# Attention in a two-layer trunk: rotation sums in token order, a third place for the swapped halves, and output products begun during the last head

## The chip, the cores and the metric

One core of one Trainium2 chip (trn2) runs the kernel. The metric is the device time of one execution in microseconds (us). The engines are TensorE (PE in the profile; PEld is its weight load), VectorE (DVE), ScalarE (ACT), GpSimd (POOL) and SyncE (SP), which issues nearly all DMAs of this kernel. The profile also gives the clock that TensorE was granted, as a share of 2.4 GHz: 1.00 is 2.4 GHz and 0.50 is 1.2 GHz.

## The reference

A trunk of two layers over 1024 tokens and 1024 channels. Layer 0 mixes tokens by a gated linear recurrence, layer 1 by dilated attention; a SwiGLU feed-forward layer (FFN) follows each, and a norm stands ahead of each part and at the end. The change touches layer 1's mixer:

```
DILATED_GROUPS = ((128, 1), (512, 4), (2048, 16))     # (window, dilation), 4 heads of 128 each

def apply_rope(x, cos, sin):
    x1, x2 = jnp.split(xf, 2, axis=-1)
    out = jnp.concatenate([x1 * cos - x2 * sin, x2 * cos + x1 * sin], axis=-1)

def dilated_attention_mixer(u, w_qkv, w_out, cos, sin):
    q = apply_rope(qkv[:, :, 0], cos, sin)
    k = apply_rope(qkv[:, :, 1], cos, sin)
    v = qkv[:, :, 2]
    for gi, (window, dilation) in enumerate(DILATED_GROUPS):
        o_g, lse_g = dilated_window_group(q[:, :, hs], k[:, :, hs], v[:, :, hs], window, dilation)
    o = jnp.stack(outs, axis=2)
    alpha = jax.nn.softmax(lse, axis=2)               # shares of the three groups
    o = (o * alpha[..., None]).reshape(B, S, ATTN_WIDTH)
    return o @ w_out

h = x
for layer in range(DEPTH):
    h = h + mixer(rmsnorm(h))
    h = h + (silu(gate) * up) @ w_down                # gate, up = rmsnorm(h) @ w_in
```

## The kernel before

Channels lie on the 128 partitions and tokens along the row. Every float32 product is made of three products of split operands (a high and a low part): a copy on ACT makes the high part, a subtraction on DVE the low one. In the profiled run the stages are: recurrence until 480 us, its output projection until 620, FFN 0 until 1290, values for all heads until about 1437, the twelve attention heads until 1756, the seam where the heads run out and the output projection starts, until 1804, the rest of that projection until 1920, and FFN 1 until the end.

A head is named by its number: n is group times 4 plus j, and the heads run in the order 0, 4, 8, 1, 5, 9, 2, 6, 10, 3, 7, 11 (j is the outer loop), so a10 is followed by a3 and a11 is the last. Head n's q and k come from seven products, a{n}a to a{n}g (twelve matmuls each, a Strassen-like scheme over the two token halves). Four of them need a copy first: L744 copies product a's sum into the bank in which c goes on adding, so **c cannot start before L744**; L750 does the same for e; L747 copies product b's sum into `s5`, half of a tile `sz{n}`.

`attn_qk` then rotates four quarters with `rope`, in the order q's first token half, k's second, q's second, k's first. A rotation copies the lower 64 rows of a quarter to the upper 64 and back (L780, L781, ACT) into `z`, the other half of `sz{n}`; `z` is multiplied by the sine table (L784), the quarter by the cosine table (L783 or L786), and L787 adds the two into the result tile `aq{n}` or `ak{n}`. Quarters 2 and 3 need `s5` added first (L778). In groups 1 and 2 the result has its tokens sorted by their remainder mod 4 or 8, "permuted" below; L778 writes permuted, so the copies L780 and L781 of quarters 2 and 3 read permuted and write back in token order, and the cosine product works on permuted data. All four rotations use the one `z`.

The steps of a head that follow are put between the products of the next: `later(n, step)` files a step under a clock that `tick()` counts, seven to a head. They are: scores (L846, into banks `as`) with their maxima (L849, DVE, into `st`) in two parts; `ng` (L856, DVE), the negative maxima; the exponentials (L858, ACT), which need `ng`; transposes (L891, PE) with copies (L892, ACT); the value products (L901) with copies (L903 or L907, ACT). After each third head the softmax sums are brought to a common layout by DMAs through memory (`dn`, `cm`), group shares are worked out (`ae`, `dw`), and the **merge** multiplies finished outputs by them: reloads L955 and L956 into `mg`, multiply L962, write L963 to `od`.

At the seam the nine merged outputs of j below 3 are loaded from `od` into tiles `am`, split into `aov0` to `aov8` (L144 on ACT, L145 on DVE) and multiplied by output weights `n3w` (L124, L125, L127): `part_out(d, lo, hi)` runs products lo to hi of unit d, six matmuls each, and two units d0 and d1 are begun among the last head's steps. The last three outputs, `aov9` to `aov11`, follow the chain `dn`, `cm`, `ae`, `dw`, a load `wb` (L1022) and a multiply (L1023); after them come products 9 to 11 of d0 and d1, and `mixer_out` with the other units.

What the engines run in order is not the written order: the framework's list scheduler sets an order for each engine from dependencies, priorities by place in the program, and its own cost estimates; an engine then takes its instructions strictly in that order. Tiles of one tag rotate through a fixed number of places: "vc" tiles hold `sz`, `aq`, `ak`, `am` and others, "wx" has two. `lm` is a mask of the recurrence in layer 0.

Of the kernel before, what the change touches and what calls it, by code (L numbers as in the profile page):

```python
# [8 lines left out]
F32 = mybir.dt.float32  # L9
F32R = mybir.dt.float32r  # L10
U8 = mybir.dt.uint8
# [4 lines left out]
P = 128  # L16
T = 1024
# [3 lines left out]
NH = 12  # L21
# [8 lines left out]
NMASK = 3 * len(STAGES) + 1  # L30
# [10 lines left out]
def trunk_kernel(ctx, tc, x, cols, consts, w_in, w_hout, w_qkv, w_aout, w_ffn, w_down, out):  # L41
    nc = tc.nc
# [8 lines left out]
    def big(tag, name, dt=F32):  # L51
        return gp.tile([P, T], dt, tag=tag, name=name, bufs=slots[tag])
# [4 lines left out]
    def mmps(name):  # L57
        return pmm.tile([P, 512], F32, tag="mm", name=name)
# [4 lines left out]
    def hs(hh):  # L63
        return slice(hh * 512, hh * 512 + 512)
# [74 lines left out]
    def split(src, tag, name, scale=None, cuts=((0, T),)):  # L139
        hi = big(tag, f"{name}h", F32R)  # L140
        lo = big(tag, f"{name}l", F32R)
        for a, b in cuts:
            if scale is None:
                nc.scalar.copy(hi[:, a:b], src[:, a:b])  # L144
                nc.vector.tensor_sub(lo[:, a:b], src[:, a:b], hi[:, a:b].bitcast(F32))  # L145
            else:
                nc.scalar.activation(hi[:, a:b], src[:, a:b], AF.Copy, scale=scale)
                nc.vector.scalar_tensor_tensor(lo[:, a:b], src[:, a:b], scale, hi[:, a:b].bitcast(F32), ALU.mult, ALU.subtract)
        return hi, lo
# [64 lines left out]
        nm.begin()  # L214
        rb = nm.finish("vb")

    lm = cp.tile([P, NMASK, 2, P], U8, name="lm")
    for i0 in range(0, NMASK, 8):
        n = min(8, NMASK - i0)
        lmf = big("ws", f"lmf{i0}")  # L220
# [498 lines left out]
    def later(n, step):  # L719
        steps.setdefault(n, []).append(step)  # L720
# [8 lines left out]
    mark = {}  # L729
# [38 lines left out]
    nc.sync.dma_start(ev0, consts[:, K_DIAG:K_DIAG + P].rearrange("(r i) c -> i r c", r=2))  # L768
    nc.vector.tensor_copy(even.rearrange("p (i r) -> p r i", r=2), ev0.rearrange("p (r i) -> p r i", r=2))

    def rope(t, ps, s5, hh, z, dil):
        tv, src, zn, cv = t[:, hs(hh)], ps[:], z, cb[:, hs(hh)]
        if dil > 1:
            n = 512 // dil
            tv = t.rearrange("p (r i) -> p i r", r=dil)[:, hh * n:hh * n + n, :]
            src, zn, cv = [y.rearrange("p (i r) -> p i r", r=dil) for y in (src, z, cv)]
        if s5 is not None:
            nc.vector.tensor_add(tv, src, s5.rearrange("p (i r) -> p i r", r=dil) if dil > 1 else s5)  # L778
            src = tv
        nc.scalar.copy(zn[0:64], src[64:128])  # L780
        mark["act"] = nc.scalar.copy(zn[64:128], src[0:64])  # L781
        if s5 is None:
            nc.vector.tensor_mul(tv, src, cv)  # L783
        nc.vector.tensor_mul(z, z, sb[:, hs(hh)])  # L784
        if s5 is not None:
            nc.vector.tensor_mul(tv, src, cv)  # L786
        mark["dve"] = nc.vector.tensor_add(tv, tv, zn)  # L787

    def qk_weights(j, gi):
        n = gi * 4 + j  # L790
        ga = load_raw(w_qkv[n], D, f"aq{n}")
        up = load_raw(w_qkv[NH + n], D, f"ak{n}", "wx")
        return pair_weights(ga, up, f"a{n}")

    def attn_qk(j, gi, w):
        n = gi * 4 + j
        sz = big("vc", f"sz{n}")
        s5, z = sz[:, 0:512], sz[:, 512:T]
        p = pair(w, qops, s5, f"a{n}")
        q = big("vc", f"aq{n}")  # L800
        k = big("vc", f"ak{n}")
        dil = (1, 4, 8)[gi]
        rope(q, next(p), None, 0, z, dil)
        rope(k, next(p), s5, 1, z, dil)
        rope(q, next(p), s5, 1, z, dil)
        rope(k, next(p), None, 0, z, dil)
        for _ in p:
            pass
        return q, k
# [140 lines left out]
    def attn_merge(j, gi):  # L950
# [13 lines left out]

        return apply

    dws = {}

    def shares(j, cv):
# [1 line left out]
            dws[j] = attn_shares(j, cv)  # L971

    sts = [sp.tile([P, 3, 8, 2], F32, tag="st", name=f"st{j}", bufs=2) for j in range(4)]
    qw = {heads[0]: qk_weights(*heads[0])}
    for i, (j, gi) in enumerate(heads):
        if i + 1 < NH:
# [19 lines left out]
        later(at + 11, lambda values=values, vv=vv: values(vv[0]))  # L996


    ov, begun, aw = [], {}, {}
    for i, (j, gi) in enumerate(heads[:9]):  # L1000
        o = big("vc", f"am{j}_{gi}")
        nc.sync.dma_start(o[:], od[gi * 4 + j])
        ov.append(split(o, "va" if i < 8 else "vb", f"aov{i}"))

    def part_out(d, lo, hi):
        if d not in begun:
            begun[d] = [mmps(f"p_n3{d}_{hh}") for hh in range(2)]
        i = lo // 6
        if (d, i) not in aw:
            aw[d, i] = load_w(w_aout[d][:, i * 768:i * 768 + 768], 768, f"n3w{d}_{i}")  # L1010
        mm3(begun[d], *aw[d, i], (lo - 6 * i) * P, ov[lo:hi], first=(lo == 0), last=(hi == NH))

    d0, d1 = DORDER[:2]
    at = clock[0]
    for upto, d, lo, hi in ((1, d0, 0, 3), (4, d0, 3, 6), (4, d0, 6, 9), (10, d1, 0, 6), (11, d1, 6, 9)):
        while clock[0] <= at + upto:
            tick()
        part_out(d, lo, hi)
    for gi in range(3):
        o = late[gi]  # L1020
        wb = big("wr", f"wb{gi}")
        nc.sync.dma_start(wb[:], dws[3][gi].partition_broadcast(P))  # L1022
        nc.vector.tensor_mul(o[:], o[:], wb[:])  # L1023
        ov.append(split(o, "vb", f"aov{9 + gi}"))
    for d in (d0, d1):
        part_out(d, 9, NH)

    ops, nm = mixer_out(1, hd[2], hd[1], ov, 2, "n3", begun)
    act1 = dp.tile([NF, P, T], F32, name="act1")
# [114 lines left out]
```

## Time and profile before

| | us |
|---|---|
| median of three runs | 2598.98 |
| lowest and highest | 2597.77, 2600.58 |
| the profiled execution | 2598.84 |
| its span in the trace | 2597.0 |

| engine | busy us | share of the span |
|---|---|---|
| PE | 2515.2 | 97% |
| DVE | 1768.1 | 68% |
| ACT | 924.1 | 36% |
| POOL | 123.5 | 5% |

All times in the trace count from the start of the span. The page of the profile lists 79% of the chain that ended last on PE, 11% on DVE, 4% on ACT and 3% on DMA. Its row of 40 slices shows PE at 9 tenths or more but for six slices, of which the 23rd, 24th and 26th (1428 to 1558 and 1623 to 1688 us) lie in the heads and the 28th at the seam, and the granted clock below 9 tenths in one slice only, the 28th (from 1753 us, the seam). A row of a timeline gives start, duration, engine, line, operation, the tile written, the tiles read, and in square brackets how long the engine stood idle before it and what it waited for.

### The profile page before, as it was taken

What the parts mean: (1) busy time and instruction counts of PE and PEld (TensorE: products, weight loads), DVE (VectorE), ACT (ScalarE), POOL (GpSimd) and SP (SyncE); (2) the same over time, 40 slices, a digit from 0 to 9 for tenths busy, and PEclk for the clock granted to TensorE, in tenths of its full rate; (3) what the DMA queues carried; (4) which work ended last, traced back from release to release, by engine and by line L of the source; (5) the groups of instructions that cost most, each with busy time, mean ns of one, the idle gap of its engine ahead of it and who ended that gap; (6) DMA issues with size and microseconds to landing.
All of it is one profiled execution on the core that took longest, in us unless ns stands there. A gap on an engine that the chain in (4) does not pass through costs nothing.

```text
span 2597.0 us, 30588 instructions
## 1 busy us (share of the span) xinstructions
PE 2515.2 (97%) x11804; PEld 2095.2 (81%) x11804; DVE 1768.1 (68%) x3079; ACT 924.1 (36%) x1400; POOL 123.5 (5%) x107
## 2 busy tenths in 40 slices
PE   8999999999999999999999889898999999999998
PEld 6888888788888888788888778776878888888887
DVE  7888888977777877433613777775477777775336
ACT  5222222244323323222523666655242333232212
POOL 1111111111000000000000000000010000000000
PEclk9999999999999999999999999998999999999999
DMA  3111111132222223532223234445322222236323
GB/s 144 33 33 33 33 33 33 41 133 94 82 89 82 81 83 130 201 102 68 93 90 111 58 98 139 130 132 164 129 80 90 73 90 82 86 100 230 109 59 127
DMA packets 113761, 246.78 MB, mean 95 GB/s; under 512 B 23632, under 2 KB 50640, under 8 KB 113616
## 3 DMA queue, kind: packets, MB, share of 16 engines
q1 hardware_dynamic: 113616, 244.83, 29.0%
q8 instruction: 93, 1.52, 0.2%
q14 instruction: 52, 0.43, 0.1%
HBM read 189.07 MB, written 55.72 MB: 94 GB/s over the span
## 4 chain that ended last, share of the span: by engine, by line
PE 79%; DVE 11%; ACT 4%; DMA 3%; issue 2%; POOL 1%; SPq 0%; DVEq 0%; POOLq 0%; ACTq 0%
PE pt L483 6%; PE pt L485 6%; PE pt L484 6%; PE pfw L125 6%; PE pfw L127 6%; PE pfw L124 6%; PE pb L484 4%; PE pb L485 4%; PE pb L483 4%; PE p_n L124 2%; PE p_n L125 2%; PE p_n L127 2%; PE pv L658 2%; PE pv L656 2%; PE pv L657 2%
## 5 line engine op out<-in xcount | busy, mean ns | idle before, releaser
L565 DVE TENSOR_TENSOR h<-pfw,h 128x512 f32<-128x512 f32 (+1 forms) x104 | 63.6, 646 | 197.5 <-PE pfw L127 197.4
L108 ACT CAST h_fw<-r_fw 128x896 fp32r<-128x896 f32 (+1 forms) x60 | 58.3, 972 | 237.9 <-PE pfw L125 219.2
L108 ACT CAST h_fa<-r_fg 128x1024 fp32r<-128x1024 f32 x44 | 46.5, 1056 | 200.0 <-PE pt L484 185.1
L108 ACT CAST h_fb<-s 128x1024 fp32r<-128x1024 f32 x44 | 46.4, 1054 | 171.1 <-PE pb L484 159.5
L342 DVE COPY_PREDICATED at<-lm,lv 128x192 f32<-128x192 uint8 (+2 forms) x288 | 82.0, 352 | 4.7 <-PE lv L327 3.7
L657 PE MATMUL pv<-vw,qb 128*128 128x512 f32 x192 | 74.8, 390 | 0.0
L656 PE MATMUL pv<-vw,qb 128*128 128x512 f32 x192 | 74.8, 390 | 0.0
L658 PE MATMUL pv<-vw,qb 128*128 128x512 f32 x192 | 74.7, 389 | 0.0
L496 DVE TENSOR_TENSOR s<-r_fu 128x512 f32<-128x512 f32 x44 | 30.3, 691 | 64.3 <-DMA r_fu<-in_w_ffn_dram 64.2
L156 POOL TENSOR_TENSOR rs_n<-ms_n,half 128x8 f32<-128x8 f32 (+2 forms) x7 | 9.3, 1334 | 1360.8 <-DVE ms_n L154 1360.8
L484 PE MATMUL pb<-n3b,h_fa 128*128 128x512 f32 x176 | 68.7, 390 | 2.6 <-DVE n3b L458 2.6
L109 DVE TENSOR_TENSOR l_fw<-r_fw,h_fw 128x896 fp32r<-128x896 f32 (+1 forms) x60 | 67.1, 1120 | 5.0 <-ACT h_fw L108 4.5
L484 PE MATMUL pb<-n1b,h_fa 128*128 128x512 f32 x176 | 68.6, 390 | 1.2 <-DVE n1b L458 1.2
L483 PE MATMUL pb<-n3b,h_fa 128*128 128x512 f32 x176 | 68.8, 391 | 0.7 <-ACT n3b L457 0.7
L483 PE MATMUL pt<-n3t,h_fb 128*128 128x512 f32 x176 | 68.9, 391 | 0.0
L483 PE MATMUL pb<-n1b,h_fa 128*128 128x512 f32 x176 | 68.6, 390 | 0.0
L483 PE MATMUL pt<-n1t,h_fb 128*128 128x512 f32 x176 | 68.6, 390 | 0.0
L484 PE MATMUL pt<-n3t,h_fb 128*128 128x512 f32 x176 | 68.5, 389 | 0.0
L485 PE MATMUL pb<-n1b,l_fa 128*128 128x512 f32 x176 | 68.5, 389 | 0.0
L485 PE MATMUL pb<-n3b,l_fa 128*128 128x512 f32 x176 | 68.5, 389 | 0.0
L485 PE MATMUL pt<-n3t,l_fb 128*128 128x512 f32 x176 | 68.5, 389 | 0.0
L485 PE MATMUL pt<-n1t,l_fb 128*128 128x512 f32 x176 | 68.5, 389 | 0.0
(1505 smaller groups left out, 7888.2 us busy)
## 6 DMA issues: line engine op xcount, KB each, us to landing
r_fu<-in_w_ffn_dram SPq DMA_DIRECT2D x44, 512.0 KB, 3.6
r_fg<-in_w_ffn_dram SPq DMA_DIRECT2D x44, 512.0 KB, 3.6
act<-g SPq DMA_DIRECT2D x44, 512.0 KB, 2.6
st<-act SPq DMA_DIRECT2D x44, 512.0 KB, 4.4
r_fw<-in_w_down_dram SPq DMA_DIRECT2D x44, 448.0 KB, 3.4
h<-hd SPq DMA_DIRECT2D x16, 512.0 KB, 5.6
r_fw<-in_w_down_dram SPq DMA_DIRECT2D x16, 512.0 KB, 3.6
vr<-in_w_qkv_dram SPq DMA_DIRECT2D x24, 256.0 KB, 3.2
```

The costliest lines, as they stand in the source:

```text
L108: nc.scalar.copy(hi[:, a:b], src[:, a:b])
L109: nc.vector.tensor_sub(lo[:, a:b], src[:, a:b], hi[:, a:b].bitcast(F32))
L124: nc.tensor.matmul(p[:, 0:b - a], wh, vh[:, a:b], start=(first and i == 0), stop=False)
L125: nc.tensor.matmul(p[:, 0:b - a], wh, vl[:, a:b], start=False, stop=False)
L127: nc.tensor.matmul(p[:, 0:b - a], wl, vh[:, a:b], start=False, stop=(last and i == n - 1))
L342: nc.vector.copy_predicated(av[:, :, d:4, :], mk[:, :, d:4, :], pv[:, :, s0:s0 + 4 - d, :])
L483: nc.tensor.matmul(ps[:], wh, bh, start=(kk == 0), stop=False)
L484: nc.tensor.matmul(ps[:], wh, bl, start=False, stop=False)
L485: nc.tensor.matmul(ps[:], wl, bh, start=False, stop=(kk == 3))
L656: nc.tensor.matmul(ps[:], vh, wh, start=(kb == 0), stop=False)
L657: nc.tensor.matmul(ps[:], vh, wl, start=False, stop=False)
L658: nc.tensor.matmul(ps[:], vl, wh, start=False, stop=(kb == 7))
```

## The change

It has four parts, all in layer 1's attention but for the mask.

1. `rope` is written anew. The sum of quarters 2 and 3 with `s5` (L776 after) is written in token order: for quarter 2 into a new tile `lz{n}`, for quarter 3 into `s5` itself. The copies (L778, L779 after) and the cosine product (L791) then read and write token order; only the last add (L794) writes permuted. Quarters 1 and 4, which have no sum, are as before.
2. `z` has two places: quarters 1, 2 and 4 use half of `sz{n}`, quarter 3 uses `lz{n}` once quarter 2 is through with it. The place for `lz` is shared with the mask `lm`, which moves to another pool.
3. `outputs(lo, hi)` loads and splits merged outputs. Outputs 0 to 3 are now filed among the last head's steps, at clocks 81 and 83 of 84; the first six of them are loaded through the two "wx" tiles and not through "vc".
4. A third unit, d2, gets two banks of the pool that holds scores and transposes. Its products 0 to 5 are written ahead of the last three outputs, its products 6 to 11 behind those of d0 and d1.

```diff
-    lm = cp.tile([P, NMASK, 2, P], U8, name="lm")
+    lm = gp.tile([P, NMASK, 2, P], U8, tag="lz", name="lm", bufs=1)
...
-    def rope(t, ps, s5, hh, z, dil):
-        tv, src, zn, cv = t[:, hs(hh)], ps[:], z, cb[:, hs(hh)]
+    def rope(t, ps, s5, y, hh, z, dil):
+        tv, zn, cv = t[:, hs(hh)], z, cb[:, hs(hh)]
+        src = ps[:]
+        if s5 is not None:
+            nc.vector.tensor_add(y, src, s5)
+            src = y
+        nc.scalar.copy(z[0:64], src[64:128])
+        mark["act"] = nc.scalar.copy(z[64:128], src[0:64])
         if dil > 1:
             n = 512 // dil
             tv = t.rearrange("p (r i) -> p i r", r=dil)[:, hh * n:hh * n + n, :]
-            src, zn, cv = [y.rearrange("p (i r) -> p i r", r=dil) for y in (src, z, cv)]
-        if s5 is not None:
-            nc.vector.tensor_add(tv, src, s5.rearrange("p (i r) -> p i r", r=dil) if dil > 1 else s5)
-            src = tv
-        nc.scalar.copy(zn[0:64], src[64:128])
-        mark["act"] = nc.scalar.copy(zn[64:128], src[0:64])
+            zn = z.rearrange("p (i r) -> p i r", r=dil)
         if s5 is None:
+            if dil > 1:
+                src, cv = [w.rearrange("p (i r) -> p i r", r=dil) for w in (src, cv)]
             nc.vector.tensor_mul(tv, src, cv)
+            y = tv
         nc.vector.tensor_mul(z, z, sb[:, hs(hh)])
         if s5 is not None:
-            nc.vector.tensor_mul(tv, src, cv)
-        mark["dve"] = nc.vector.tensor_add(tv, tv, zn)
+            nc.vector.tensor_mul(y, y, cv)
+            if dil > 1:
+                y = y.rearrange("p (i r) -> p i r", r=dil)
+        mark["dve"] = nc.vector.tensor_add(tv, y, zn)
...
-        s5, z = sz[:, 0:512], sz[:, 512:T]
+        s5, z1 = sz[:, 0:512], sz[:, 512:T]
+        z2 = gp.tile([P, 512], F32, tag="lz", name=f"lz{n}", bufs=1)[:]
...
-        rope(q, next(p), None, 0, z, dil)
-        rope(k, next(p), s5, 1, z, dil)
-        rope(q, next(p), s5, 1, z, dil)
-        rope(k, next(p), None, 0, z, dil)
+        rope(q, next(p), None, None, 0, z1, dil)
+        rope(k, next(p), s5, z2, 1, z1, dil)
+        rope(q, next(p), s5, s5, 1, z2, dil)
+        rope(k, next(p), None, None, 0, z1, dil)
...
+    def outputs(lo, hi):
+        for i in range(lo, hi):
+            j, gi = heads[i]
+            o = big("wx" if i < 6 else "vc", f"am{j}_{gi}")
+            nc.sync.dma_start(o[:], od[gi * 4 + j])
+            ov.append(split(o, "va" if i < 8 else "vb", f"aov{i}"))
...
+    later(7 * NH - 3, lambda: outputs(0, 2))
+    later(7 * NH - 1, lambda: outputs(2, 4))
...
-    for i, (j, gi) in enumerate(heads[:9]):
-        o = big("vc", f"am{j}_{gi}")
-        nc.sync.dma_start(o[:], od[gi * 4 + j])
-        ov.append(split(o, "va" if i < 8 else "vb", f"aov{i}"))
...
-            begun[d] = [mmps(f"p_n3{d}_{hh}") for hh in range(2)]
+            begun[d] = [(axps if d == d2 else mmps)(f"p_n3{d}_{hh}") for hh in range(2)]
...
-    d0, d1 = DORDER[:2]
+    outputs(4, 9)
+    d0, d1, d2 = DORDER[:3]
...
+    part_out(d2, 0, 6)
...
+    part_out(d2, 6, NH)
```

Three places in the order. The first is on ACT, where a10's rotations end and a3 begins. `ap` and `ng` are the exponentials' tiles, those of a6 (12151, 12158); `sz`, `aq` and `r_ak` are a10's, `a10g` is the split of its last weights, and L744 is a3's. Before:

```order
L858 ACTIVATE ap_1_12151,st_10657<-ap_1_12151,ng_12329 128x256 x2
L858 ACTIVATE ap_1_12151,st_10657<-ap_1_12151,ng_12329 128x128
L780 COPY sz_12181<-aq_12182 64x512
L781 COPY sz_12181<-aq_12182 64x512
L613 CAST a10g<-r_ak_12154 128x512
L744 COPY p_a_12416<-p_a_12414 128x512
L780 COPY sz_12181<-p_a_12187 64x512
L781 COPY sz_12181<-p_a_12187 64x512
L613 CAST a3a<-r_aq_12382 128x512
```

After (L866 is the exponentials' line, L778 and L779 are the copies):

```order
L866 ACTIVATE ap_1_12158,st_10657<-ap_1_12158,ng_12337 128x256 x2
L866 ACTIVATE ap_1_12158,st_10657<-ap_1_12158,ng_12337 128x128
L778 COPY lz_12189<-sz_12188 64x512
L779 COPY lz_12189<-sz_12188 64x512
L613 CAST a10g<-r_ak_12161 128x512
L778 COPY sz_12188<-p_a_12195 64x512
L779 COPY sz_12188<-p_a_12195 64x512
L744 COPY p_a_12425<-p_a_12423 128x512
L613 CAST a3a<-r_aq_12390 128x512
```

The copies of a10's third rotation now read `sz` (its `s5` half) and write `lz`; those of its fourth stand ahead of a3's L744 and not behind it.

The second place is on DVE, in a3, where the maxima of a10 end (`as`, `st`) and `ng` releases its exponentials. `aq`, `ak`, `sz` and `lz` are a3's, `a3e` is the low part of a weight split. The four maxima of the last bank of scores repeat, and one of them is shown. Before:

```order
L778 TENSOR_TENSOR ak_12413<-p_a_12417,sz_12411 128x64x8
L849 ISA ap_1_12381,st_10657<-as_0_12562,kon 128x128
L849 ISA st_10657 128x1
...
L856 TENSOR_SCALAR ng_12571<-st_10657 128x8
L784 TENSOR_TENSOR sz_12411<-sz_12411,sb 128x512
L786 TENSOR_TENSOR ak_12413<-ak_12413,cb 128x64x8
L787 TENSOR_TENSOR ak_12413<-ak_12413,sz_12411 128x64x8
L778 TENSOR_TENSOR aq_12412<-p_a_12416,sz_12411 128x64x8
L614 TENSOR_TENSOR a3e<-r_aq_12382,a3e 128x512
```

After (L857 is the maxima's line, L864 that of `ng`, L776 the sums with `s5`, L789 and L791 the products by sine and cosine, L794 the last add):

```order
L776 TENSOR_TENSOR lz_12420<-p_a_12426,sz_12419 128x512
L857 ISA ap_1_12389,st_10657<-as_0_12571,kon 128x128
L857 ISA st_10657 128x1
...
L789 TENSOR_TENSOR sz_12419<-sz_12419,sb 128x512
L791 TENSOR_TENSOR lz_12420<-lz_12420,cb 128x512
L857 ISA ap_1_12389,st_10657<-as_0_12571,kon 128x128
...
L794 TENSOR_TENSOR ak_12422<-lz_12420,sz_12419 128x64x8
...
L776 TENSOR_TENSOR sz_12419<-p_a_12425,sz_12419 128x512
L864 TENSOR_SCALAR ng_12580<-st_10657 128x8
L614 TENSOR_TENSOR a3e<-r_aq_12390,a3e 128x512
```

Of a3's rotations the second one's two products and last add, and the third one's sum, now stand between the maxima and ahead of `ng`, which stood ahead of them.

The third place is on ACT in the last head, a11, whose L744, L747 and L750 these are; `apx` are the transposes of a7. Before:

```order
L744 COPY p_a_13081<-p_a_13079 128x512
L780 COPY sz_12875<-p_a_12881 64x512
L781 COPY sz_12875<-p_a_12881 64x512
L747 COPY sz_13076<-p_a_13080 128x512
L750 COPY p_a_13082<-p_a_13081 128x512
L892 COPY ap_0_12844<-apx_1_0_13132 128x512
L892 COPY ap_0_12844<-apx_3_2_13138 128x512
L108 CAST h_n3w_0_13348<-r_n3w_0_13346 128x768
L780 COPY sz_13076<-p_a_13079 64x512
```

After (L900 copies the transposes):

```order
L779 COPY sz_12885<-p_a_12892 64x512
L744 COPY p_a_13093<-p_a_13091 128x512
L144 CAST aov0h<-am_0_13218 128x1024
L747 COPY sz_13087<-p_a_13092 128x512
L144 CAST aov1h<-am_1_13224 128x1024
L750 COPY p_a_13094<-p_a_13093 128x512
L900 COPY ap_0_12854<-apx_1_0_13144 128x512
L900 COPY ap_0_12854<-apx_3_2_13150 128x512
L108 CAST h_n3w_0_13360<-r_n3w_0_13358 128x768
L144 CAST aov2h<-am_2_13313 128x1024
L144 CAST aov3h<-am_0_13319 128x1024
L778 COPY sz_13087<-p_a_13091 64x512
```

Four casts of the split outputs now stand among the last head's copies. On PE, eighteen products of `aov0` to `aov2` come right behind a11g and ahead of the transposes they followed; thirty-six products of d2 come ahead of the first of `aov9`, and d2's other thirty-six behind those of d0 and d1. The mask's move changes no row.

## Rows read from the trace of the kernel before

**Rows 1.** Windows: start:end, length, busy us (instructions) by engine, clock, DMA share, GB/s.

```profile
620.00:1023.00 403.00, 403.00 (x1788) 333.99 (x1787) 313.43 (x387) 127.37 (x154) 1.64 (x1) 1.00 0.25 84
1437.00:1756.00 319.00, 287.62 (x1432) 239.81 (x1432) 235.14 (x488) 195.15 (x408) 0.00 (x0) 0.97 0.37 112
1756.00:1804.00 48.00, 37.17 (x182) 29.39 (x183) 25.14 (x47) 27.18 (x53) 0.00 (x0) 0.90 0.50 157
1660.90:1664.30 3.40, 3.40 (x10) 2.64 (x9) 2.02 (x11) 2.74 (x5) 0.00 (x0) 0.50 0.98 339
```

**Rows 2.** PE's waits in 1437 to 1832: us in total, times, longest us.

```profile
PE p_a L712 <- ACT p_a L744: 13.8, 6, 4.1
PE as L846 <- DVE ak L787: 10.2, 7, 2.6
...
PE p_n L124 <- ACT aov0h L144: 4.3, 1, 4.3
```

**Rows 3.** Tile `sz`: duration ns min/median/max, first and last start, forms.

```profile
L784 DVE TENSOR_TENSOR sz<-sz,sb x48: 670/688/694, 1423.3 to 1766.0; 128x512 f32<-128x512 f32 x48
L780 ACT COPY sz<-p_a x24: 582/584/587, 1421.4 to 1763.9; 64x512 f32<-64x512 f32 x24
...
L778 DVE TENSOR_TENSOR ak<-p_a,sz x12: 682/1047/1062, 1425.7 to 1746.3; 128x512 f32<-128x512 f32 x12
L780 ACT COPY sz<-ak x12: 617/1100/1137, 1426.5 to 1747.4; 64x512 f32<-64x512 f32 x12
```

**Rows 4.** Timelines of DVE, ACT and PE, a10 into a3: start, us, instruction, idle before.

```profile
1627.90 0.69 DVE L784 TENSOR_TENSOR sz<-sz,sb 128x512 f32<-128x512 f32 x1 [1.10 <-ACT sz L781]
...
1631.17 0.17 DVE L856 TENSOR_SCALAR ng<-st 128x8 f32<-128x8 f32 x1
...
1635.86 1.08 ACT L780 COPY sz<-aq 64x512 f32<-64x512 f32 x1
...
1639.21 0.50 PE L712 MATMUL p_a<-qt,a10c 128*128 128x512 f32 x1 [2.73 <-ACT p_a L744]
...
1646.00 1.99 PE L846 MATMUL as<-ak,aq 128*128 128x256 f32 x8 [1.30 <-DVE ak L787]
```

**Rows 5.** Chain of waits (first row), then timelines of DVE, ACT, PE, a3.

```profile
1651.11 4.23 DMA mg<-dw
...
1662.22 0.17 DVE L856 TENSOR_SCALAR ng<-st 128x8 f32<-128x8 f32 x1
...
1671.49 0.58 ACT L744 COPY p_a<-p_a 128x512 f32<-128x512 f32 x1
...
1678.68 1.49 PE L846 MATMUL as<-ak,aq 128*128 128x128 f32 x11 [1.62 <-DVE ak L787]
```

**Rows 6.** Timeline of PE: products c and scores in a8, a1 and a2.

```profile
1462.52 0.50 PE L712 MATMUL p_a<-qt,a8c 128*128 128x512 f32 x1 [4.09 <-ACT p_a L744]
...
1468.85 0.48 PE L846 MATMUL as<-ak,aq 128*128 128x256 f32 x1 [0.85 <-DVE ak L787]
...
1493.65 0.50 PE L712 MATMUL p_a<-qt,a1c 128*128 128x512 f32 x1 [1.34 <-ACT p_a L744]
...
1499.31 0.82 PE L846 MATMUL as<-ak,aq 128*128 128x128 f32 x5 [1.72 <-DVE ak L787]
...
1588.27 0.82 PE L846 MATMUL as<-ak,aq 128*128 128x128 f32 x5 [2.59 <-DVE ak L787]
```

**Rows 7.** Timeline of PE, and the chain (third row): last head and seam.

```profile
1748.02 0.38 PE L846 MATMUL as<-ak,aq 128*128 128x128 f32 x1 [1.70 <-DVE st L849]
...
1768.65 0.33 PE L846 MATMUL as<-ak,aq 128*128 128x128 f32 x1
...
1784.33 5.06 DMA dn<-st
...
1803.36 1.22 PE L124 MATMUL p_n<-aov9h,h_n3w 128*128 128x512 f32 x2 [5.08 <-ACT aov9h L144]
...
1829.95 0.39 PE L124 MATMUL p_n<-aov0h,h_n3w 128*128 128x512 f32 x1
```

More of the change, by code (lines that the diff above doesn't have):

```diff
@@ L965, in attn_merge @@
         return apply
+    ov, begun, aw = [], {}, {}
+    def outputs(lo, hi):
[4 more added lines that the diff above has]
+            ov.append(split(o, "va" if i < 8 else "vb", f"aov{i}"))
     dws = {}
@@ L996, in trunk_kernel @@
         later(at + 11, lambda values=values, vv=vv: values(vv[0]))
-    ov, begun, aw = [], {}, {}
-    for i, (j, gi) in enumerate(heads[:9]):
-        o = big("vc", f"am{j}_{gi}")
-        nc.sync.dma_start(o[:], od[gi * 4 + j])
-        ov.append(split(o, "va" if i < 8 else "vb", f"aov{i}"))
     def part_out(d, lo, hi):
         if d not in begun:
-            begun[d] = [mmps(f"p_n3{d}_{hh}") for hh in range(2)]
+            begun[d] = [(axps if d == d2 else mmps)(f"p_n3{d}_{hh}") for hh in range(2)]
         i = lo // 6
```

## The prediction

> **What bounds the kernel now.** I read the stage table first [rows 1]. In the FFN stretch at 620 us TensorE (PE) is busy for all 403.00 us at full clock: what sets the time there is PE's own work, and the change adds and takes none. In the attention stretch it is busy 287.62 of 319.00 us, clock 0.97; at the seam, where attention hands over to the output projection, 37.17 of 48.00 us, clock 0.90. So 31.4 + 10.8 = 42.2 us idle, and 3% of 319 and 10% of 48, 9.6 + 4.8 = 14.4 us, of clock: some 56 us bound any gain. The clock row at 1660.9 shows its price: 3.40 us at 0.50, the 1.2 GHz level, with PE working all through, so 1.7 us lost. Such stretches follow PE's longer waits.
>
> Then who ends PE's waits [rows 2]. Six times product c waits for ScalarE's (ACT's) copy L744 that seeds it: 13.8 us. Seven times the scores L846 wait for the last add of k's rotation on VectorE (DVE): 10.2 us. At the seam PE waits 4.3 us for the first split output and 5.1 us for the tenth [rows 7]. The first two are ACT and DVE in series, not PE; there the rope edit works. The last two are the seam, where the other edits work.
>
> **The rope edit, walked at a10.** Durations first [rows 3]. A copy of 64 rows out of k costs 617 ns where k lies in token order (dilation 1) and 1100 ns where it is permuted; the first add 682 against 1047 ns. After the change both read and write token order in all heads; only the last add still writes permuted. The Trainium skill (VectorE: DVE Perf Modes, Mode 1× (REGULAR) — the baseline) has the baseline mode give one result a cycle and says "fp32, weird strides, PSUM operands — all work"; by it the DVE half of this saving would be nothing. The 682 to 1047 ns of the same line differ, so I take the rows; the rule is a rival below.
>
> Now the place [rows 4]. In a6 (dilation 4) DVE waits 1.10 us for the second copy at 1627.90, and at 1631.17 it makes ng, which releases the exponentials. After: the first add 0.3 us sooner, two copies 0.5 us shorter each, the product by cos 0.4 us shorter, less 0.1 us of overlap. Ng comes 1.6 us sooner, and the exponentials with it. Behind them now stand two permuted copies (from 1635.86), a split and L744, which lets c go at 1639.21: 3.35 us. After stand two copies of 0.5 us less each, and two more of the fourth rotation, 0.6 us each: some 3.7 us. So c gains 1.1 us, rounded down, and its wait of 2.73 us shrinks to 1.6 us; I take it that such a wait no longer brings half clock behind it, which gives 1.7 us. The fourth rotation no longer waits for the third, because z has two halves; by the same durations its last add ends at 1641.2, before PE has done c and the transposes, so the scores' wait of 1.30 us before 1646.00 goes. In sum 4.0 us by then.
>
> Part of that is given back in a3 [rows 5]. The merge's write leaves 4 us sooner, and its reload lands at 1651 (now 1651.11 + 4.23 = 1655.34). But the order puts the whole second rotation and the third's first add ahead of ng. From the landing to ng it is now 6.9 us (until 1662.22). After it is the same plus a split 0.7, a product by sin 0.7, one by cos 0.7, a strided add 1.0, an add 0.7 and a wait for two copies 1.3, or 12.0: ng at 1663.0, no sooner than now. Exponentials, split, one short copy and two copies later L744 starts at 1670.4 (now 1671.49), while PE is ready for it near 1666: a new wait of 4 to 5 us, half clock behind it. The scores come at 1676.3 where they now come at 1678.68. The pair a10, a3 thus gains 2.4 us and not 8.
>
> The other pairs by the same walk [rows 6]: a9 and a2 gain 1.4 us at the scores at 1588.27, and 1.7 us more since the half clock behind their 2.59 us wait goes: 3.1. Before a8 and a1 stands no merge: c of a8 comes 1.0 sooner (its wait of 4.09 us hardly shrinks), the scores' wait of 0.9 goes, and in a1 ng precedes the third add, so 1.34 and 1.72 us go: 5.0. Sum 10.5 us. From both sides: were nothing put ahead of ng, the two merge pairs would gain 8 each (+11); were the reloads no sooner than now, they would lose 4 each (-13).
>
> **The last head and the seam** [rows 7]. Six loads of merged outputs now go through the two "wx" buffers and stand in SyncE's queue among the merge's writes and loads; their splits, 1024 columns each, so by twice the 512-column rows some 1.2 us on ACT and 1.4 on DVE [rows 3], stand between L744, L747, L750 and the rotation's copies. Two of these copies wait for a load that waits for a buffer, so the transposes' copies come some 2 us late and PE idles 1.8 us before the value products; the scores at 1748.02 come at 1747.5, so the 4.0 us won before them are given back but for 0.5. Behind them it pays: PE runs 18 products of aov0 to aov2 where it now waits 4.3 us, and the scores at 1768.65 come at 1765.6, since the copies ahead are short and fewer splits follow. From these scores to the last exponential it is now 15.7 us (the write dn leaves at 1784.33); with the splits gone ahead I put 13.6, so 1779.2. From there to the tenth split the chain of four DMAs is unchanged: 1803.36 - 1784.33 = 19.0, so 1798.2. PE meanwhile has 36 products of the second unit, 18 more, eight value products and now 36 of the third unit. At 403.00/1788 = 0.225 us each [rows 1] that is 8.1 + 4.1 + 1.8 + 8.1 = 22.1, until 1801.9 with the remaining transposes. So the 5.1 us wait goes, and the 72 products that then remain for three units end at 1818.1; now the third unit ends at 1829.95. That is 11.8 us, less one or two half-clock stretches behind waits for aov6 and the exponentials: 9.5. Nothing late behind it: the third unit's second weights need a buffer that the second wb multiply frees, near 1799, and land well before 1810 if they take the merge reload's 4.2 us [rows 5]. From both sides: 13 if no split stalls ACT; 3 if only the last wait goes. The mask's move to the other pool changes no row of any engine.
>
> **Sum.** 10.5 + 9.5 = 20.0 us. The profiled execution took 2598.84 (median of the runs 2598.98), so 2578.8; I say 2579.
>
> **Rivals.**
> - *The early walk holds* (20%). Ng is not late in a2 and a3, since the copies and the third add are done beside the reload's landing; then the merge pairs gain 8 each. For it: DVE is idle in part of that stretch. Against: DVE takes its rows in order. 2579 - 11 - 4 (the last head's copy of the place) = 2564.
> - *The seam gives nothing* (22%). Loads through two buffers in series with their splits hold ACT in the last head, and the scores there come no sooner. For it: the load is on a stretch where the DMAs are busy 0.98 of the time around 1660.9 and 0.50 at the seam [rows 1]. The last wait of 5.1 still goes, less what the head loses: 2579 + 7 = 2586.
> - *Strides cost nothing on DVE* (3%). Then each ng comes 0.8 us later than walked, in six passages: 2579 + 5 = 2584. This is the skill's baseline-mode rule above; the rows speak against it.
> - *Nothing moves* (7%): every wait taken from the scores comes back at the seeded product, as in a3, and the seam as in the second rival: 2596.
> - *Slower* (5%). The place is the merge's reload in a9, a10 and the last head: with six loads and earlier weight loads in flight it lands later than now by x. Ng is 12 us behind it and L744 behind ng, so each place loses 4 + x more than I walked, 3(4 + x). It decides from x = 2.7 us on, where 20 us are used up; at x = 4 the time is 2579 + 24 = 2603. Against: the reload's own release comes 4 us sooner at two of the three.
>
> **Chances and range.** The forecast has 43% and by itself spans 2573 to 2584. With the first two rivals' times inside and the unknown bounds, 2562 to 2591 holds the time 8 in 10. What this kernel's measurement can tell from no change is about 0.2%, 5.2 us, so faster means below 2593.8: 43 + 20 + 22 + 3 = 0.88; same 0.07; slower 0.05.
>
> **What would show it.** Right: scores wait for k's last add below 2 us in sum (10.2 now); no PE wait for aov9; the wait for L744 gone in a1 but 3 us and more in a2 and a3, with ng there following the third rotation's first add; copies of 64 rows from the sum all near 620 ns. Wrong: c in a2 and a3 without a wait (then 2564 is nearer), or PE in the last head waiting longer than now before the values and second scores (then 2586), or reloads of the merge landing later than now against the write before them (then slower). A split of the first outputs that waits for its load on ACT while PE stands at product d or e would show my seam term too large.

## The result, and the profile after

| | before | after |
|---|---|---|
| median us | 2599.5 (4 runs, 2597.77 to 2600.58) | 2567.64 (4 runs, 2565.24 to 2570.81) |
| profiled execution, its span | 2598.84, 2597.0 | 2565.24, 2563.3 |
| ratio | | 0.9879 (0.9862 to 0.9896) |

The change made the kernel 31.9 us faster where 20 were forecast; 2567.64 lies inside the range of 2562 to 2591, but below the 2573 to 2584 that the forecast by itself spans. The sum was made against the profiled execution, and by the spans of the two profiles the gain is 33.7 us.

One correction first. The words ahead of the order rows, and the heading of [rows 4], name some heads one too late. In the first place on ACT the exponentials are a2's, the rotations a6's, and `a10g` and L744 are a10's; in the second, on DVE, the maxima and `ng` are a6's and the rotations a10's; in the third `apx` are the transposes of a3; [rows 4] leads from a6 into a10. The prediction's walk itself follows the rows.

The stage windows of after, columns as in [rows 1]; the third is a stretch in a3:

```profile
1437.00:1756.00 319.00, 298.76 (x1531) 250.79 (x1529) 241.32 (x522) 198.04 (x439) 0.00 (x0) 0.98 0.44 131
1756.00:1804.00 48.00, 47.58 (x221) 39.10 (x220) 26.64 (x38) 22.73 (x42) 2.58 (x2) 1.00 0.48 146
1655.95:1662.70 6.75, 4.97 (x12) 3.91 (x13) 6.75 (x11) 2.79 (x6) 0.00 (x0) 0.50 0.72 230
```

In the heads PE is busy 298.8 of 319 us (287.6 before), at the seam 47.6 of 48, and the seam's clock is 1.00 (0.90 before). The same view over the whole of attention and seam, of before and then of after:

```profile
1430.00:1835.00 405.00, 362.80 (x1773) 300.56 (x1772) 287.53 (x569) 241.95 (x489) 2.59 (x2) 0.96 0.40 124
```

```profile
1430.00:1835.00 405.00, 384.34 (x1918) 321.35 (x1917) 285.12 (x583) 233.43 (x499) 5.15 (x4) 0.98 0.44 133
```

PE is idle 21.5 us less. The clock is 0.98 and not 0.96; the trace's record of the granted clock has three stretches at 0.50 there (13.7 us together) where before it had eight (34.1 us), and half of the difference, 10.2 us, is time won. Idle and clock together are 31.7 of the 33.7 us; another 1.1 us was won behind the output projection, in single short waits.

PE's waits of after in the same window as [rows 2], with us in total, times, longest:

```profile
PE p_a L712 <- ACT p_a L744: 15.4, 6, 4.0
PE apo L909 <- ACT ap L900: 1.9, 2, 1.1
PE as L854 <- DVE st L857: 1.6, 1, 1.6
PE as L854 <- DVE ak L794: 0.9, 2, 0.5
```

The scores' wait for k's last add is 0.9 us and was 10.2; that for product c stays the largest, 15.4 us. No row names the first or the tenth split output any more. Durations on the new tile `lz`, columns as in [rows 3]:

```profile
L776 DVE TENSOR_TENSOR lz<-p_a,sz x12: 669/680/684, 1425.8 to 1727.4; 128x512 f32<-128x512 f32 x12
L778 ACT COPY sz<-lz x12: 616/618/619, 1426.6 to 1729.1; 64x512 f32<-64x512 f32 x12
...
L794 DVE TENSOR_TENSOR ak<-lz,sz x12: 691/1084/1108, 1429.8 to 1732.6; 128x512 f32<-128x512 f32 x12
```

The sums take 680 ns and the copies out of them 618 ns in all heads. The add that still writes permuted takes 1084 ns.

How the lead grew: the start of a product's first matmul in the trace, before minus after, in us (profiled executions; the right-hand columns belong to the experiments).

| up to | after | rope_only | seam_only | permuted | seed_not11 |
|---|---|---|---|---|---|
| a5a, past a8 and a1 | 6.4 | 4.8 | 0.2 | 1.2 | 9.7 |
| a6a, past a9 and a2 | 11.1 | 8.5 | 0.3 | -0.1 | 17.3 |
| a11a, past a10 and a3 | 15.4 | 12.5 | -0.7 | -1.8 | 22.6 |
| a11g | 17.6 | 18.6 | -5.5 | -7.0 | 23.9 |
| end of the span | 33.7 | 19.7 | 6.4 | 7.0 | 38.7 |

The heads of after and of rope_only have one and the same rotation, and 15.4 and 12.5 us at a11a; a second profile of the changed kernel had 12.5. Counted from the first product of a8, six profiles with these same rows in the heads (after, its second profile after_again, rope_only, no_third, no_early, vc_late) gained 12.9 to 15.4 us. So differences of 2 to 3 us between single profiles say nothing, and 15.4 is the most of the six.

### The profile page after: what moved, and what is told of

Read it like the earlier page. It is cut to its first block, busy times and chain, and to the rows that moved or that the text cites. A ratio compares the mean times of both kernels' runs of the same rounds, so it can differ in the third digit from the quotient of the medians.

```text
span 2563.3 us, 30583 instructions
## 1 busy us (share of the span) xinstructions
PE 2505.7 (98%) x11804; PEld 2089.4 (82%) x11804; DVE 1754.9 (68%) x3079; ACT 907.8 (35%) x1400; POOL 123.6 (5%) x107
## 4 chain that ended last, share of the span: by engine, by line
PE 82%; DVE 9%; ACT 3%; DMA 2%; issue 2%; POOL 1%; SPq 0%; DVEq 0%; POOLq 0%; ACTq 0%
PE pt L485 6%; PE pt L484 6%; PE pt L483 6%; PE pfw L125 6%; PE pfw L127 6%; PE pfw L124 6%; PE pb L484 4%; PE pb L485 4%; PE pb L483 4%; PE p_n L125 2%; PE p_n L127 2%; PE p_n L124 2%; PE pv L657 2%; PE pv L658 2%; PE pv L656 2%
```

## The experiments

The order of the runs is that of the questions: which edit, which part of it, and whether the new wait is one for data.

**Each edit alone.** rope_only takes the kernel before and puts in the change's hunks of `lm`, `rope` and `attn_qk`:

```diff
-        rope(k, next(p), s5, 1, z, dil)
-        rope(q, next(p), s5, 1, z, dil)
+        rope(k, next(p), s5, z2, 1, z1, dil)
+        rope(q, next(p), s5, s5, 1, z2, dil)
```

> Only the rotation's edit (token-order sums, the second place for the swapped halves, the mask's move); outputs and units at the seam as before. My theory, that the edits act at places of their own: at the first product of a11 the run is 15.4 us ahead of the kernel before, as the changed kernel is; without splits among the last head's copies it is 19 to 20 us ahead at a11g; the seam's two waits (4.3 and 5.1 us) and its half clock stay. 2580 us. Rival, that the rotation's gain in the heads is small without the seam's edits behind it (what is won is lost again in the seam's waits): 2590 us or more.

Measured: 2577.53 us, ratio 0.9918 (0.9903 to 0.9933); 20 us faster than before on its chip, 2597.48. seam_only is its counterpart, the changed kernel with these hunks taken back:

```diff
-        rope(k, next(p), s5, z2, 1, z1, dil)
-        rope(q, next(p), s5, s5, 1, z2, dil)
+        rope(k, next(p), s5, 1, z, dil)
+        rope(q, next(p), s5, 1, z, dil)
```

> Only the seam's edits (first outputs split early, third unit begun), with the rotation of before. My theory: nothing moves before a10's products, and the seam gives 14 us by itself, since its waits for the first and the tenth split output (4.3 and 5.1 us) and two stretches at half clock go: 2586 us. Rival, that the early splits need the room which the short copies make on ACT, and otherwise hold the last head's copies: 2592 us, with waits before the last head's products of 5 us and more.

Measured: 2588.44 us, ratio 0.9963 (0.9949 to 0.9977), 9 us faster. PE's waits of rope_only from 1437 to 1832 us, then of seam_only:

```profile
PE p_a L712 <- ACT p_a L744: 15.4, 6, 4.0
PE p_n L124 <- DVE ak L786: 4.6, 1, 4.6
PE p_n L124 <- ACT aov9h L144: 1.9, 1, 1.9
```

```profile
PE as L847 <- DVE ak L788: 16.8, 8, 2.9
PE p_a L712 <- ACT p_a L744: 14.0, 7, 4.1
PE as L847 <- DVE st L850: 6.2, 3, 3.4
```

In rope_only the heads won what they win in the changed kernel. At the seam the wait for the first split output stays, 4.6 us (the row names DVE's product on `ak`, which ends at 1743.61; the cast of `aov0h` ends at 1743.59), with 13.7 us at 0.50 behind the two waits there; that for the tenth fell from 5.1 to 1.9 us. In seam_only neither expectation holds whole: the seam wins, but the last head loses first. From its PE timeline in a11, the value products, and the scores that answer to those at 1748.02 in [rows 7]:

```profile
1744.99 3.62 PE L902 MATMUL apo<-ap,avv 128*128 128x128 f32 x30 [1.22 <-ACT ap L893]
1751.96 1.16 PE L847 MATMUL as<-ak,aq 128*128 128x128 f32 x8 [3.35 <-DVE st L850]
```

From a11a to a11g it loses 4.8 us against the kernel before (-0.7 to -5.5): these waits are 1.22 and 3.35 us where there were none and 1.70, and 3.4 us at 0.50 follow. The longest waits for k's last add, 2.9 us, are in a9 and a10 and not there. So the early splits do hold the last head; they hold it with short copies too, where a11g comes 29.5 us behind a11a in after, 31.9 in after_again, and 25.9 and 25.6 in vc_late and rope_only, which have no early splits. From a11a to the end of the span the seam's edits alone bring 7.1 us (-0.7 to 6.4 in the table), the rotation's alone 7.2 (12.5 to 19.7), and both together 16 to 18 (15.4 to 33.7, and 12.5 to 28.4 in the second profile). Whether each helps the other there isn't shown: the 2 to 4 us between are hardly more than profiles of the same rows differ by, and in the medians 20.0 + 9.0 = 29.0 against 31.9 lies within the intervals.

**Inside the rotation.** one_place gives the third rotation the place of the others:

```diff
-        rope(q, next(p), s5, s5, 1, z2, dil)
+        rope(q, next(p), s5, s5, 1, z1, dil)
```

> The changed kernel with one place for the swapped halves: the third rotation uses the same half of sz as the others. My theory, that both halves of the rotation's edit count, this one by letting the fourth rotation go before the third: waits of the scores for k's last add come back in a9, a10 and a11 with 0.5 to 1 us each, while L744 stands one pair of copies earlier there and its wait of 1.26 us goes; in sum 2 to 5 us more, 2570 us. Rival, that the second place brings most of the rotation's 20 us: 2580 us.

Measured: 2570.39 us, ratio 0.9887 (0.9871 to 0.9902), which the changed kernel's interval overlaps. permuted keeps both places and takes the whole `rope` of before:

```diff
-            nc.vector.tensor_add(y, src, s5)
-            src = y
+            nc.vector.tensor_add(tv, src, s5.rearrange("p (i r) -> p i r", r=dil) if dil > 1 else s5)
+            src = tv
...
-        rope(q, next(p), s5, s5, 1, z2, dil)
+        rope(q, next(p), s5, 1, z2, dil)
```

> The changed kernel with two places, but the sums written permuted as before, so that the copies read permuted data. My theory: two copies of 1100 instead of 620 ns and an add of 1047 instead of 682 ns stand ahead of L744 and of the last add in groups 1 and 2; L744's waits in a9, a10, a11 grow from 1.26 to 2.3 us, each with half clock behind it (1.7 us), and those in a2 and a3 by 1 us: 11 us more, 2579 us. Rival, the page's rule that strides cost DVE nothing, by which only the copies count: 6 us more, 2574 us, and the first add at 682 ns either way.

Measured: 2589.17 us, ratio 0.9963 (0.9953 to 0.9974), 21 us slower than the changed kernel; about what the seam's edits give alone. Waits of one_place, then of permuted:

```profile
PE as L854 <- DVE ak L794: 13.7, 7, 2.5
PE p_a L712 <- ACT p_a L744: 3.2, 2, 2.8
```

```profile
PE p_a L712 <- ACT p_a L744: 28.2, 7, 5.3
PE as L848 <- DVE st L851: 4.4, 1, 4.4
```

Two places without short copies bring nothing: 28.2 us of waits for L744. With the second place the fourth rotation's copies go ahead of L744, and these and two permuted ones are 3.4 us; the scores' waits turned into waits for c. Short copies with one place leave the order of before, with scores waiting 13.7 us and c 3.2, and cost only 2.8 us against after, too little to be told from none. That is the time expected for one_place, but not the waits: those of the scores were to come back with at most 3 us and are 13.7, while those of c fell from 15.4 to 3.2. So the token order carries nearly all of the rotation's gain, and the second place by itself none that can be told. I had expected 11 us and not 21: the waits in a9, a10 and a11 were to grow from 1.26 to 2.3 us and are 3.9. In a10 L744 starts 2.7 us later against the head's first product than in after. The third rotation's two longer copies behind the exponentials make 0.9 us of that; the other 1.8 us are `ng`, which waits for the second rotation's longer sum, copies and cosine product; that I had not counted. The spans of the two profiles differ by 26.7 us; from 1430 to 1835 us PE is idle 16.7 us more, and the clock takes 10.2 us more (34.1 us at 0.50 against 13.7). Durations in permuted:

```profile
L779 DVE TENSOR_TENSOR ak<-p_a,sz x12: 684/1047/1084, 1425.4 to 1750.5; 128x512 f32<-128x512 f32 x12
L781 ACT COPY sz<-ak x12: 617/1104/1137, 1426.2 to 1752.4; 64x512 f32<-64x512 f32 x12
```

The same sum is 1047 ns here and 680 ns in token order, the copy 1104 and 618.

**Inside the seam.** no_third leaves out the third unit's early products:

```diff
-    part_out(d2, 0, 6)
...
-    part_out(d2, 6, NH)
```

> The changed kernel without the third unit. My theory: the third unit's 36 products (8.1 us) cover the chain of four transfers to the tenth split output. Without them PE runs dry some 3.7 us before that split ends (1772.8 against 1776.5), and half clock follows, 1.7 to 3.4 us: 2573 us. Rival, that the chain is early enough and the third unit only moves work from later: 2568 us with no wait for the tenth output.

Measured: 2576.14 us, ratio 0.9911 (0.9896 to 0.9926), 8.5 us slower than the changed kernel. Timeline of its PE at the tenth output, and the clock behind it:

```profile
1781.03 0.80 PE L124 MATMUL p_n<-aov9h,h_n3w 128*128 128x512 f32 x1 [3.85 <-ACT aov9h L144]
...
1780.84:1784.24 3.40, 3.21 (x8) 2.56 (x9) 2.74 (x3) 1.18 (x2) 0.00 (x0) 0.50 0.87 252
```

The wait is the expected one, 3.85 us with 3.4 us at half clock, so the third unit does cover the chain; 3 us more than expected were lost, and single profiles can't tell where. no_early files all outputs behind the heads:

```diff
-    later(7 * NH - 3, lambda: outputs(0, 2))
-    later(7 * NH - 1, lambda: outputs(2, 4))
...
-    outputs(4, 9)
+    outputs(0, 9)
```

> The changed kernel with outputs 0 to 3 loaded and split after the last head's products are written, as before, but through the two buffers. My theory: the wait for the first split output comes back with 4 us and a stretch at half clock, while the last head's waits before value products and scores (1.1 and 1.6 us) go: 2572 us. Rival, that early splits cost in the last head what they bring behind it: 2567 us.

Measured: 2568.81 us, ratio 0.9887 (0.9873 to 0.9902). Neither theory was tried: by the orders of both programs, all rows of every engine stand as in the changed kernel. With the "wx" places the early filing does nothing. The places do it: by the view of the tiles `am`, the first load leaves at 1684.4 us in the changed kernel and left at 1751.2 through "vc" before. So vc_late takes the places away as well:

```diff
-    later(7 * NH - 3, lambda: outputs(0, 2))
-    later(7 * NH - 1, lambda: outputs(2, 4))
...
-    outputs(4, 9)
+    outputs(0, 9)
...
-            o = big("wx" if i < 6 else "vc", f"am{j}_{gi}")
+            o = big("vc", f"am{j}_{gi}")
```

> The changed kernel with the first outputs filed behind the last head and loaded through the vc places, as before the change; the run without the early filing alone had the same order as the changed kernel, so the two wx places are what moves these loads. My theory: a11's waits of 1.1 and 1.6 us go and a11g comes 2.7 us earlier; behind it the wait for the first split output is back, 4 to 5 us with up to 10 us at half clock (5 us lost), as in the run with the rotation's edit alone: 6 us lost there, 3 us in sum, 2571 us. Rival, that the early splits are worth nothing since PE has the third unit to fill in with: 2568 us or less.

Measured: 2571.30 us, ratio 0.9891 (0.9877 to 0.9906). PE's waits:

```profile
PE p_n L124 <- DVE ak L787: 4.6, 1, 4.6
PE apx L899 <- ACT ap L866: 1.0, 1, 1.0
...
PE apo L909 <- ACT ap L900: 0.8, 1, 0.8
```

The first load leaves at 1732.5 us here and at 1686.1 in no_early, from which only the place differs. In the last head nothing is lost and a11g comes 21.0 us ahead of before; behind it 4.6 us of wait and the half clock return. Time and waits are those that were expected, though the interval overlaps the changed kernel's: what the early splits bring, 2.7 to 3.7 us by the medians, can't be told from none, and the third unit (8.5 us) is the larger part of the seam's edits.

**The wait for L744.** In a2 and a3 it was forecast as a new wait. Is it one for data, or for a place in ACT's queue? seed_first gives the copy priority:

```diff
-        nc.scalar.copy(p2[:], p1[:])
+        with tc.high_priority():
+            mark["seed"] = nc.scalar.copy(p2[:], p1[:])
```

> The changed kernel with the seeding copy L744 given high priority, so that it stands ahead of the fourth rotation's copies in every head, and ahead of most of the exponentials in a8. My theory, that product c waits for L744's place in ACT's queue and not for data: the waits of 1.26 us in a9, a10, a11 go, that of 4.0 us in a8 falls under 0.5 us with the half clock behind it (1.7 us), those of 3.8 us in a2 and a3 fall to about 2 us: 13 us, 2555 us. Rival, that the copies which now stand behind it make the scores wait as much: 2566 us.

Measured: 2561.08 us, ratio 0.9849 (0.9835 to 0.9864). PE's waits:

```profile
PE as L855 <- DVE ak L795: 9.8, 7, 1.8
PE as L855 <- DVE st L858: 7.6, 3, 3.6
```

Its window over attention and seam:

```profile
1430.00:1835.00 405.00, 386.92 (x1940) 325.14 (x1939) 283.76 (x583) 233.86 (x499) 5.16 (x4) 0.99 0.45 134
```

All six waits for L744 are gone, 15.4 us, so they were for a place in the queue and not for product a's sum. But the scores wait 17.4 us where they waited 2.5: nearly all of it came back there, as the rival has it, and from 1430 to 1835 PE is idle only 2.6 us less. The rest of the gain is clock: 6.8 us at 0.50 in that stretch and not 13.7, which is 3.4 us. Together 6.0 us, where the two profiled spans differ by 5.7 and the medians by 6.6; the intervals overlap by a hair (0.9864 against 0.9862). The next two runs took the heads apart, and after_again is the changed kernel on the same chip. seed_some:

```diff
+        with (tc.high_priority() if name in ("a8", "a2", "a3") else ExitStack()):
+            nc.scalar.copy(p2[:], p1[:])
```

seed_wx3 is seed_some with

```diff
-            o = big("wx" if i < 6 else "vc", f"am{j}_{gi}")
+            o = big("wx" if i < 3 else "vc", f"am{j}_{gi}")
```

> The changed kernel with the seeding copy L744 at high priority in heads 8, 2 and 3 alone, where product c waited 4.0, 3.8 and 3.8 us. Theory: with it everywhere the stretches of a8, a2 and a3 gained 5.1, 3.9 and 4.6 us on the changed kernel's profile, while those of a9, a10 and a11 lost 3.7, 2.0 and 2.1 us to waits of the scores; in three heads alone only the gains are left, 12 to 13 us: 2555 us. Rival, that a gain in one head is given back in the next, because DVE's order shifts with it: 2561 us, as with it everywhere.

> The same, and only the first three of the merged outputs go through the two wx places, the others through the vc places. Theory: PE needs aov0 to aov2 right behind a11g and no more; the split of aov3, which held ACT for its load ahead of the last head's copies (2.35 us), then stands behind the last head's rotations, and the waits of 1.1 and 1.6 us before a11's value products and scores shrink: 2 us less than the run with heads 8, 2 and 3 alone, 2553 us. Rival, that aov3 to aov5 are then late for PE by as much: the same time, with a wait for aov3.

> The changed kernel once more beside the two others on the same chip, so that what they bring is read against it and not across chips: 2566 to 2570 us, as before; a difference of more than 5 us would mean that runs on different chips can't be compared at this size.

Measured: 2563.31 (0.9853, 0.9840 to 0.9866), 2564.25 (0.9862, 0.9849 to 0.9876) and 2568.56 us (0.9877, 0.9863 to 0.9890). PE's waits in seed_some, then the two waits of seed_wx3's last head:

```profile
PE as L855 <- DVE ak L795: 7.9, 5, 2.9
PE p_a L712 <- ACT p_a L745: 7.9, 6, 1.5
```

```profile
1742.41 0.73 PE L125 MATMUL p_n<-aov3l,h_n3w 128*128 128x512 f32 x2 [1.88 <-DVE aov3l L145]
...
1726.58 0.60 PE L855 MATMUL as<-ak,aq 128*128 128x128 f32 x3 [2.96 <-DVE st L858]
```

Adding up the good heads of two profiles failed. In seed_some a2 and a3 still wait 1.5 us for L744, and 2.9 us for the scores behind it: the scheduler placed the neighbours anew. And fewer early loads are no gain that can be told (0.9 us the other way); PE then waits 1.9 us for aov3. The rivals of both stand. The last run gives priority in all heads but the last:

```diff
+        with (ExitStack() if name == "a11" else tc.high_priority()):
+            nc.scalar.copy(p2[:], p1[:])
```

> The changed kernel with L744 at high priority in every head but the last. Theory: heads 8 to 3 keep what the run with it everywhere won (22 to 23 us ahead of the kernel before at the first product of a11), and in a11, where that run waited 3.6 us for maxima behind the rotation on DVE and gained nothing, the stretch gains the 2 us that it gains in the changed kernel: 2559 us. Rival, that the last head's loss only passes through to the seam, where the third unit's products fill in: 2561 us, no difference to the run with it everywhere.

Measured: 2558.42 us, ratio 0.9842 (0.9828 to 0.9855), where the theory had 2559; it beats both kernels, 10.1 us below the changed kernel's second measurement (9.1 by the ratios). Its waits:

```profile
PE as L855 <- DVE ak L795: 8.8, 8, 1.6
PE as L855 <- DVE st L858: 5.0, 3, 2.0
PE apo L910 <- ACT ap L901: 1.7, 1, 1.7
PE p_a L712 <- ACT p_a L745: 1.3, 1, 1.3
```

Against seed_first (0.9849) the intervals overlap, so the rival isn't excluded, and from a11a to a11g the profile gained 1.3 us and not 2; against the changed kernel (0.9862 at its lowest, 0.9863 the second time) they don't.

## Why the prediction was right, and where it was too small

**The heads: mechanism right, 10.5 us forecast, 12.9 to 15.4 in the profiles.** The walk at a10 came out nearly as written. Its wait for L744 was to shrink from 2.73 to 1.6 us without half clock behind it:

```profile
1626.63 0.50 PE L712 MATMUL p_a<-qt,a10c 128*128 128x512 f32 x1 [1.26 <-ACT p_a L744]
```

It is 1.26 us, the clock stays at full, and the scores' wait of 1.30 us is gone. The give-back in a3 came too. From its chain of waits, then PE's timeline:

```profile
1634.63 3.72 DMA mg<-dw
...
1649.38 0.60 DVE sz L776
1649.99 0.08 DVE ng L864
...
1655.38 0.62 ACT lz L779
...
1657.19 0.49 ACT p_a L744
...
1657.72 0.80 PE L712 MATMUL p_a<-qt,a3c 128*128 128x512 f32 x1 [3.80 <-ACT p_a L744]
```

The reload lands at 1638.35; `ng` follows the third rotation's sum (L776) and starts at 1649.90 in the timeline, 11.6 us after the landing where 12.0 were forecast. The chain then goes through the exponentials and three copies to L744, and c waits 3.80 us (4 to 5 forecast) with the clock at 0.50 (the third window above). Two things came out better: the reload lands 1.5 us sooner against a10's products than the walk put it, and the stretch at half clock in a10, at 1660.9 in [rows 1], went too, which the walk did not count. The pairs gained 6.4, 4.7 and 4.2 us for 5.0, 3.1 and 2.4. The profiles of after_again and no_early, whose rows are the same, give 5.7, 5.1 and 3.6, and 5.2, 4.2 and 3.8.

**The last head and the seam: 9.5 us forecast, 16 to 18 measured.** This is the term that was mis-sized. Rows of after that answer to [rows 7]:

```profile
1730.60 1.16 PE L854 MATMUL as<-ak,aq 128*128 128x128 f32 x8 [1.57 <-DVE st L857]
...
1747.64 0.35 PE L854 MATMUL as<-ak,aq 128*128 128x128 f32 x1 [0.55 <-DVE ak L794]
...
1758.91 0.53 SPq L931 DMA_DIRECT2D dn<-st  x1
...
1775.45 1.05 ACT L144 CAST aov9h<-ao 128x1024 fp32r<-128x1024 f32 x1 [5.37 <-DVE ao L1038]
...
1780.89 0.39 PE L124 MATMUL p_n<-aov9h,h_n3w 128*128 128x512 f32 x1
```

Less the 15.4 us of lead that the heads brought, the first scores come 2.1 us sooner (0.5 forecast), the second 5.7 (3.1), and the write `dn` 10.1 (5.1). In after_again these are 1.2, 4.0 and 8.1, and in no_early 2.0, 5.6 and 8.8, so the size varies but each is above its forecast. Two steps failed. The last head was to win 4.0 us before the first of these scores and to give back 3.5 to the splits. Without early splits it wins 6.0 (rope_only) and 5.8 (vc_late), so the win was put too small; the give-back, PE's waits of 1.1 us before the values and 1.6 before the scores among it, is 3.7 to 4.8 and was put about right. And from the second scores to `dn` it took 11.3 us and not 13.6: seven casts of split outputs, some 1.05 us each, stood on ACT in this stretch before, and two are left, so I had taken out too little for them. These steps, with 1.0 us between the two scores, make 4.9 us. The third step is the 2.3 us taken off for half clock: in this profile there is none from a11 to the end of the seam (none in no_early either, 3.4 us at 0.50 in after_again). 9.5 + 4.9 + 2.3 = 16.7. The last part was sized right: from `dn` to the tenth output's products PE has 22.0 us of work (22.1 forecast) and doesn't wait, while the split of `aov9` ends at 1776.5, 4.4 us before PE needs it.

**The rivals.** The early walk (2564) came nearest in time, but not by its mechanism: c does wait in a2 and a3. That rival's time is what had stretched the range below 2573, so that the range holds 2567.64 is in part luck. "The seam gives nothing" had its mechanism half right: early splits do cost the last head, 4.8 us in seam_only and 3.5 to 5.9 with short copies (after and after_again against vc_late), but behind a11g 9.2 us come back against vc_late. "Slower" needed the reloads to land later than now; they land in 3.72 us where they took 4.23 [rows 5], and sooner.

**Strides.** For the rival that strides cost DVE nothing: 1047 against 680 ns for one sum on one tile settle it. The Trainium skill (SBUF — State Buffer, Door 1: The DMA port swizzle) says that SBUF has 16-byte lines and that each access which crosses to a new line pays a penalty. The rows agree: by the patterns in `rope` permuted neighbours lie 1024 or 512 bytes apart, and a DVE add that writes them takes 1.5 times and an ACT copy that reads them 1.8 times as long (1104 against 618 ns). From the sentence on the baseline mode in the Trainium skill (VectorE: DVE Perf Modes, Mode 1× (REGULAR) — the baseline), read as one on time, they differ, and the measurement decides. The last add after the change, whose writes are permuted too, takes 1084 ns.

**A part that brings nothing.** With the "wx" places, the early filing of the first outputs moves no instruction; the choice of place does, which the prediction's walk named without asking which of the two it was.

## What to carry to other kernels

Where engines run in a fixed order, price an edit by what now stands ahead of the next thing that TensorE needs: sums in token order, with the shorter copies that follow from them, won 21 us here; a second buffer alone only moved the wait from the scores to product c. Keep data that two engines exchange in the order in which both read it, and permute once, in the last write. To make a list scheduler start a transfer early, look at whose place it takes before moving the line that issues it.

## What the hardware showed beyond expectation

How much half clock follows the waits, and how little a wait's length tells of it. Waits of 1.26 us in a9, a10 and a11 left the granted clock at 1.00; waits of 2.7 us at the same product before, and of 3.8 us in a2 and a3 after, had 0.50 behind them. But length draws no line: in one_place a wait of 2.5 us in a10 had it and one of 2.5 us in a9 had none, and in after_again the wait in a2 had none at 3.7 us.

```profile
1632.20 0.48 PE L854 MATMUL as<-ak,aq 128*128 128x256 f32 x1 [2.51 <-DVE ak L794]
...
1548.32 0.92 PE L854 MATMUL as<-ak,aq 128*128 128x256 f32 x3 [2.51 <-DVE ak L794]
...
1575.77 0.50 PE L712 MATMUL p_a<-qt,a2c 128*128 128x512 f32 x1 [3.71 <-ACT p_a L744]
```

So what such a stretch costs can be read from a profile, but these runs don't show how to forecast one. Over 1430 to 1835 us, idle time and time at 0.50 were 42.2 and 34.1 us before, 20.7 and 13.7 in the changed kernel, and 18.1 and 6.8 in seed_first, where waits are more and shorter. In that profile, waits that were moved and cut in two won more by the clock (3.4 us) than in idle time (2.6); profiles of the changed kernel's own rows differ by as much, with 17.1 us at 0.50 in after_again and 20.5 in no_early.
